# A hybrid decoder layer: the first weight group in a written order, and the stick-breaking heads' last 16 keys in one step

## The chip, the cores and the metric

The kernel runs on one core of a Trainium2 chip. The metric is the device time of one execution, in microseconds (us). Five engines run side by side: TensorE (PE), VectorE (DVE), ScalarE (ACT), GpSimd (POOL) and SyncE (SP, which here only issues DMAs).

## What is computed

One layer over 256 tokens with 16 learned meta tokens in front (T = 272 columns), model width 2048, all in float32:

```
xn = rmsnorm(h) * g_pre;  u = xn @ w_in                  # 5132 columns
mLSTM heads (6), stick-breaking heads (6), pooling (4)   # mixers, from parts of u
h += rmsnorm(concat(mixers) @ w_out);  h += rmsnorm(SwiGLU FFN(h))

stick-breaking, per head:  z = q.k / sqrt(128), keys s < t
A[t,s] = sigmoid(z_ts) * prod_{s<j<t} (1 - sigmoid(z_tj));  out_t = sum_s A[t,s] v_s
```

The keys of a head are the 272 positions, in tiles of 128, 128 and 16. Only the last 16 queries see the last 16 keys.

## The kernel before, in words

**Precision.** Each float32 weight tile is loaded raw and split into a rounded part `hi` (ACT, line 95) and a rest `lo` (DVE, line 96); a product is x_hi·w_hi + x_lo·w_hi + x_hi·w_lo. `mm3` (lines 100 to 102) issues three matmuls into the same columns; `mm2` (lines 545 and 549) takes x_hi and x_lo side by side as one 512-column matmul with `hi`, and one 256-column matmul with `lo`.

**The order of work.** `w_in` is worked through in 11 groups of three or four 128-column blocks (the table `plan`); within a group the 16 k-tiles of 128 rows come in chunks, each loaded by SP into one of three `raw` buffers, split, and multiplied into PSUM banks `acc0` to `acc3`. A block is evacuated when its 16 k-tiles are done. The recording layer schedules PE, ACT and DVE from the program's order. Between the matmuls of the groups `tick()` hands out one step of the heads' own work at a time, with waiting times counted in ticks (`LAG`, `VLAG`); that work uses four other PSUM banks, `mx()`.

**Group 0** (queries of stick-breaking heads 0 to 2, and the 12 gate columns) also makes the transposed x. `x_trans(k)` (lines 222 to 227) transposes one k-tile of the meta tokens `mt` and of both halves of `xin` into a bank; ACT and DVE turn it into `xhi` and `xlo`, scaled by the gain column `gmc`. Eight matmuls on `ones` and the transpose that makes `gmc` (lines 198 and 199) stand ahead of that. The gates use `mm3` with 38 columns of weights `gw` and 272 moving columns, once per k-tile. `x_squares` and `x_norm` make the rms factor `rb`, needed only for evacuation.

**The stick-breaking heads** run in three steps, `LAG` ticks apart: scores (lines 326 to 328, one matmul per key tile, 256, 144 and 16 columns), running sums through the triangle `tri` and `ones_r` (lines 357 to 359, for each of two parts), and weighted values (lines 332 to 334). `vals` (lines 318 to 320) transposes the values, one transpose per key tile. The mLSTM heads use the same `scores`, `weighted` and `vals`.

After `w_in` come the output projection, the FFN's gate and up products, and its down product, with the same splits; they take the time from about 300 us on.

## Time and profile before

| | |
|---|---|
| median of 3 runs | 1117.08 us (1117.01 to 1117.27) |
| profiled execution, its own time | 1117.11 us |
| its span | 1115.4 us |
| PE busy | 1103.0 us |
| DVE busy | 706.8 us |
| ACT busy | 509.6 us |

The span runs from the first to the last instruction; the execution's own time has 1.7 us around it. A line of the timeline gives an instruction's start and its duration. Matmuls overlap in the array, so what one costs PE in a stream is the distance from its start to the next one's, not its duration. The granted clock is given as a share of 2.4 GHz: 1.00 or 0.50 (1.2 GHz).

### The profile page before, as it was taken

How to read it: one execution, taken by the hardware profiler on the slowest of the kernel's cores; microseconds unless marked ns; L12 is line 12 of the kernel's file. 1: busy time of each engine (PE TensorE's matmuls, PEld its weight loads, DVE VectorE, ACT ScalarE, POOL GpSimd, SP SyncE). 2: the span in 40 equal slices, each digit the busy share in tenths (PEclk: the TensorE clock that was granted, in tenths of full speed). 3: DMA queues.
4: the chain of work that ended last, by engine and by line, in shares of the span. 5: the costliest groups of instructions: out<-in, count | busy, mean ns of one | idle time of the engine just before them, and what ended most of it. 6: DMA issues, size and time to landing. Idle time of an engine off the chain costs nothing.

```text
span 1115.4 us, 14181 instructions
## 1 busy us (share of the span) xinstructions
PE 1103.0 (99%) x5671; PEld 943.9 (85%) x5671; DVE 706.8 (63%) x942; ACT 509.6 (46%) x684; POOL 20.5 (2%) x47
## 2 busy tenths in 40 slices
PE   8999999999999999999999999999999999999997
PEld 6899999999988888888888888888888888888885
DVE  4777755868945767576575675774765844454444
ACT  6544455635434654444444444444344543343332
POOL 3000000000000000000000000000000000000000
PEclk8999999999999999999999999999999999999999
DMA  7554644544495555555655555656655565555552
GB/s 245 181 170 151 206 146 130 179 144 128 152 344 194 203 189 189 189 197 182 216 197 189 189 189 190 197 180 208 206 178 199 179 202 190 199 191 198 198 191 75
DMA packets 100545, 208.54 MB, mean 187 GB/s; under 512 B 3962, under 2 KB 31402, under 8 KB 99952
## 3 DMA queue, kind: packets, MB, share of 16 engines
q1 hardware_dynamic: 99168, 201.58, 55.0%
q0 software_dynamic: 896, 2.92, 0.9%
q10 hardware_dynamic: 416, 3.15, 0.7%
q8 instruction: 44, 0.72, 0.3%
q14 instruction: 21, 0.17, 0.0%
HBM read 205.52 MB, written 2.11 MB: 186 GB/s over the span
## 4 chain that ended last, share of the span: by engine, by line
PE 96%; DVE 2%; ACT 1%; DMA 0%; issue 0%; SPq 0%; DVEq 0%; POOLq 0%; ACTq 0%
PE mx L771 8%; PE mx L773 8%; PE mx L772 8%; PE acc L773 7%; PE acc L772 7%; PE acc L771 6%; PE acc L102 5%; PE acc L100 5%; PE acc L101 5%; PE mx L662 5%; PE mx L661 5%; PE mx L663 5%; PE acc L662 5%; PE acc L663 5%; PE acc L661 5%; PE acc L545 4%
## 5 line engine op out<-in xcount | busy, mean ns | idle before, releaser
L96 DVE TENSOR_TENSOR lo<-raw,hi 128x1024 fp32r<-128x1024 f32 (+1 forms) x384 | 458.6, 1200 | 347.4 <-ACT hi L95 345.7
L95 ACT CAST hi<-raw 128x1024 fp32r<-128x1024 f32 (+1 forms) x384 | 394.2, 1030 | 478.9 <-PE mx L773 124.6
L771 PE MATMUL mx<-hi,x 128*128 128x512 f32 x384 | 149.6, 390 | 0.0
L773 PE MATMUL mx<-hi,x 128*128 128x512 f32 x384 | 149.6, 390 | 0.0
L772 PE MATMUL mx<-lo,x 128*128 128x512 f32 x384 | 149.4, 389 | 0.0
L102 PE MATMUL acc<-x,lo 128*128 128x272 f32 (+3 forms) x448 | 132.7, 297 | 0.0
L100 PE MATMUL acc<-x,hi 128*128 128x272 f32 (+3 forms) x448 | 130.5, 292 | 0.1
L101 PE MATMUL acc<-x,hi 128*128 128x272 f32 (+3 forms) x448 | 130.6, 292 | 0.0
L771 PE MATMUL acc<-hi,x 128*128 128x512 f32 x320 | 124.5, 389 | 0.0
L772 PE MATMUL acc<-lo,x 128*128 128x512 f32 x320 | 124.5, 389 | 0.0
L773 PE MATMUL acc<-hi,x 128*128 128x512 f32 x320 | 124.5, 389 | 0.0
L101 PEld LDWEIGHTS acc<-x,hi 128*128 128x128 f32 x448 | 84.4, 188 | 0.7
L100 PEld LDWEIGHTS acc<-x,hi 128*128 128x128 f32 x448 | 84.3, 188 | 0.8 <-DVE sbq L507 0.3
L771 PEld LDWEIGHTS mx<-hi,x 128*128 128x128 f32 x384 | 72.1, 188 | 15.1 <-ACT x L864 0.3
L773 PEld LDWEIGHTS mx<-hi,x 128*128 128x128 f32 x384 | 72.1, 188 | 15.0
L102 PEld LDWEIGHTS acc<-x,lo 128*128 128x128 f32 x448 | 84.4, 189 | 0.4
L772 PEld LDWEIGHTS mx<-lo,x 128*128 128x128 f32 x384 | 72.1, 188 | 14.8
L802 DVE STREAM_TRANSPOSE turn<-hg 32x256 f32<-32x256 f32 x176 | 76.7, 436 | 2.8
L545 PE MATMUL acc<-x,hi 128*128 128x512 f32 x192 | 73.1, 415 | 0.7 <-DVE x L227 0.3
L772 PEld LDWEIGHTS acc<-lo,x 128*128 128x128 f32 x320 | 60.1, 188 | 12.5
L771 PEld LDWEIGHTS acc<-hi,x 128*128 128x128 f32 x320 | 60.1, 188 | 12.5
L773 PEld LDWEIGHTS acc<-hi,x 128*128 128x128 f32 x320 | 60.1, 188 | 12.4
(253 smaller groups left out, 1468.4 us busy)
## 6 DMA issues: line engine op xcount, KB each, us to landing
raw<-in_w_gate_up_dram SPq DMA_DIRECT2D x88, 1024.0 KB, 5.0
raw<-in_w_down_dram SPq DMA_DIRECT2D x44, 1024.0 KB, 5.3
raw<-in_w_in_dram SPq DMA_DIRECT2D x36, 512.0 KB, 4.8
raw<-in_w_out_dram SPq DMA_DIRECT2D x16, 1024.0 KB, 6.0
raw<-in_w_in_dram SPq DMA_DIRECT2D x12, 1024.0 KB, 5.2
raw<-in_w_in_dram SPq DMA_DIRECT2D x8, 768.0 KB, 4.5
raw<-in_w_in_dram SPq DMA_DIRECT2D x3, 792.0 KB, 7.6
h<-in_x_dram ACTq DMA_DIRECT2D x1, 2048.0 KB, 13.2
```

The source lines that it names most:

```text
L95: act.copy(out=h, in_=r)
L96: vec.tensor_tensor(out=l, in0=r, in1=h.bitcast(F32), op=ALU.subtract)
L100: pe.matmul(o, lhsT=wh, rhs=xh, start=start, stop=False, **kw)
L101: pe.matmul(o, lhsT=wh, rhs=xl, start=False, stop=False, **kw)
L102: pe.matmul(o, lhsT=wl, rhs=xh, start=False, stop=stop, **kw)
L545: pe.matmul(o, lhsT=wh, rhs=xx[:, :, k, NMETA:], start=k == 0, stop=k == KT - 1, skip_group_check=True)
L661: pe.matmul(o, lhsT=lh, rhs=h[:, 0, js], start=k == 0, stop=False)
L662: pe.matmul(o, lhsT=lh, rhs=l[:, 0, js], start=False, stop=False)
L663: pe.matmul(o, lhsT=ll, rhs=h[:, 0, js], start=False, stop=k == nk - 1)
L771: pe.matmul(o, lhsT=x2hi[:, k, ts], rhs=h[:, kk, :], start=k == 0, stop=False)
L772: pe.matmul(o, lhsT=x2hi[:, k, ts], rhs=l[:, kk, :], start=False, stop=False)
L773: pe.matmul(o, lhsT=x2lo[:, k, ts], rhs=h[:, kk, :], start=False, stop=k == KT - 1)
```

## The change

**Group 0** is written out by hand (`first_group`), and PE, ACT and DVE keep that order. Its loads have buffers of their own: the three `raw` buffers hold two pairs of k-tiles each, and two of the heads' slots hold the last two pairs. SP issues x and weights in turn, the meta tokens after the sixth; the gain row moves to ACT's queue and `pool_w` behind group 0. The meta tokens are loaded as 128 rows (8 k-tiles by 16 tokens) and transposed twice in all instead of once per k-tile. The gate weights `hi` and `lo` lie side by side, so the gates take two matmuls per k-tile instead of three; ACT and DVE add the parts later. Group 0 is evacuated in the middle of group 1 (`late`), and group 1, now of three blocks, accumulates in three of the four `mx` banks. `mm2` takes `hi` first except in the last k-tile.

**The last 16 keys** of the six stick-breaking heads are gathered by POOL into `q3`, `k3` and `vt3` (96 columns, 16 per head). `last_keys` does their scores and running sums in one step under a block mask, `last_values` one transpose, `last_sums` one product that is added to the heads' last 16 queries. The heads themselves drop their third key tile and subtract the totals `tot3` with one small DVE operation.

```diff
-    chunks = {}
-
-    def load0(a, b):
-        chunks[a] = load(win_view(a, b - a, OG, 396), b - a, 396)
-
-    sp.dma_start(out=row0, in_=g_mix_pre.rearrange("o (a b) -> (o a) b", b=P))
-    load_x(0, 2)
-    sp.dma_start(out=mt, in_=meta)
-    load0(0, 2)
-    load_x(2, 4)
-    load0(2, 4)
-    load_x(4, 8)
-    load0(4, 8)
-    load_x(8, 12)
-    load_x(12, 16)
...
+    raw0 = {}
+    for c in range(3):
+        raw = rawp.tile([P, 2 * MB], F32, tag="raw", name=nm("raw"), bufs=RAWB)
+        for h in range(2):
+            raw0[4 * c + 2 * h] = raw[:, h * 792 : (h + 1) * 792]
+    for h in range(2):
+        raw0[12 + 2 * h] = slots0[1 + h][:, :792]
+    raw0 = {k: r.rearrange("p (k c) -> p k c", c=396) for k, r in raw0.items()}
+
+    def load0(k):
+        sp.dma_start(out=raw0[k], in_=win_view(k, 2, OG, 396))
+
+    act.dma_start(out=row0, in_=g_mix_pre.rearrange("o (a b) -> (o a) b", b=P))
+    for a, b in ((0, 2), (2, 4), (4, 8), (8, 12), (12, 16)):
+        load_x(a, b)
+        for k in range(a, b, 2):
+            load0(k)
+        if b == 8:
+            for h in range(2):
+                sp.dma_start(out=mt8[:, h, :],
+                             in_=meta[:, h * 1024 : (h + 1) * 1024].rearrange("t (k c) -> k t c", c=P))
...
-    pool.dma_start(out=pw, in_=pool_w[0].rearrange("g c d -> c g d"))
...
+    gw = big.tile([P, KT, P], F32R, tag="mixlo", name="gw")
+    pool.memset(gw.bitcast(F32), 0.0)
...
-    pc = mx()
-    for _ in range(8):
-
-        pe.matmul(pc[:, :P], lhsT=ones, rhs=ones, start=True, stop=True)
-    pe.transpose(pc[:, :16], row0, ident[:16, :16])
-    vec.tensor_copy(out=gmc, in_=pc[:, :16])
...
+    def gain_column():
+        pc = mx()
+        warm(pc, 5)
+        pe.transpose(pc[:, :16], row0, ident[:16, :16])
+        vec.tensor_copy(out=gmc, in_=pc[:, :16])
+        warm(pc, 6)
...
-        pe.transpose(pt[:, 0:NMETA], mt[:, ks], ident[:NMETA, :NMETA])
-        pe.transpose(pt[:, NMETA : NMETA + P], xin[:, 0, ks], ident)
-        pe.transpose(pt[:, NMETA + P : T], xin[:, 1, ks], ident)
+        pe.transpose(pt[:, 0:P], xin[:, 0, ks], ident)
+        pe.transpose(pt[:, P : 2 * P], xin[:, 1, ks], ident)
...
-        act.activation(xhi[:, k, :], pt[:, :T], AF.Identity, scale=g)
-        vec.scalar_tensor_tensor(out=xlo[:, k, :], in0=pt[:, :T], scalar=g, in1=xhi[:, k, :].bitcast(F32),
+        act.activation(xhi[:, k, NMETA:], pt[:, :NT], AF.Identity, scale=g)
+        vec.scalar_tensor_tensor(out=xlo[:, k, NMETA:], in0=pt[:, :NT], scalar=g, in1=xhi[:, k, NMETA:].bitcast(F32),
                                  op0=ALU.mult, op1=ALU.subtract)
...
+    def meta_trans():
+        pt = mx()
+        act.activation(jk[:, : 2 * P], mt8.rearrange("p h c -> p (h c)"), AF.Square, accum_out=ssx[:, 2, 0:1])
+        for h in range(2):
+            pe.transpose(pt[:, h * P : (h + 1) * P], mt8[:, h, :], ident)
+        mg = itile(NT).rearrange("p (k t) -> p k t", t=NMETA)
+        vec.tensor_tensor(out=mg, in0=pt[:, : 2 * P].rearrange("p (k t) -> p k t", t=NMETA),
+                          in1=gmc.unsqueeze(2).broadcast_to([P, KT, NMETA]), op=ALU.mult)
+        act.copy(out=xhi[:, :, 0:NMETA], in_=mg)
+        vec.tensor_tensor(out=xlo[:, :, 0:NMETA], in0=mg, in1=xhi[:, :, 0:NMETA].bitcast(F32), op=ALU.subtract)
...
+    def meta_sums():
+        pt = mx()
+        pe.matmul(pt[:NMETA, 0:2], lhsT=sel, rhs=ssx[:, 2, :], start=True, stop=True)
...
+        act.copy(out=e[F], in_=pg[96:102, :T])
+        act.copy(out=ig[:NH], in_=pg[64:70, :T])
...
-        pe.transpose(pv[:, 2 * P : 3 * P], vt[:, K2:T], ident)
-        act.copy(out=dst, in_=pv[:, 0 : 3 * P].rearrange("p (a b) -> p a b", b=P))
...
+        n = dst.shape[1]
+        if n == 3:
+            pe.transpose(pv[:, 2 * P : 3 * P], vt[:, K2:T], ident)
+        act.copy(out=dst, in_=pv[:, 0 : n * P].rearrange("p (a b) -> p a b", b=P))
...
+
+    def scores(k, q, three=True):
         pz = mx()
...
+    have = {"qk": 0, "v": 0, "tot": False, "heads": 0}
+
+    def last_keys():
+        zm, s = zm3[:L16], part3[:L16]
+        pz = mx()
+        pe.matmul(pz[:L16, :L16], lhsT=k3, rhs=q3, start=True, stop=True)
+        vec.tensor_tensor(out=zm, in0=pz[:L16, :L16], in1=sbm3, op=ALU.add)
+        softplus(s, zm)
+        act.copy(out=s3[0], in_=s)
+        vec.tensor_tensor(out=s3[1], in0=s, in1=s3[0].bitcast(F32), op=ALU.subtract)
+        yield
+        pr = mx()
+        for j in range(2):
+            pe.matmul(pr[:, L16 : 2 * L16], lhsT=ones_r[:L16], rhs=s3[j], start=j == 0, stop=False, skip_group_check=True)
+        for j in range(2):
+            pe.matmul(pr[:L16, :L16], lhsT=tri3, rhs=s3[j], start=False, stop=j == 1, skip_group_check=True)
+        vec.tensor_tensor(out=zm, in0=zm, in1=pr[:L16, :L16], op=ALU.subtract)
+        vec.tensor_copy(out=tot3, in_=pr[:, L16 : 2 * L16])
+        act.activation(zm, zm, AF.Exp)
+        have["tot"] = True
+
+    def last_values():
+        pv = mx()
+        pe.transpose(pv[:L16, :P], vt3, ident)
+        vec.tensor_copy(out=v3, in_=pv[:L16, :P])
+        yield
+
+    def last_sums():
+        mhi, mlo_ = mix_tiles()
+        po = mx()
+        pe.matmul(po[:, :L16], lhsT=v3, rhs=zm3[:L16], start=True, stop=True)
+        vec.tensor_tensor(out=part3, in0=po[:, :L16], in1=part3, op=ALU.add)
+        hi, lo = (m[:, NH : 2 * NH, 240:256] for m in (mhi, mlo_))
+        p3 = part3.rearrange("p (h t) -> p h t", t=16)
+        act.copy(out=hi, in_=p3)
+        vec.tensor_tensor(out=lo, in0=p3, in1=hi.bitcast(F32), op=ALU.subtract)
+        ready.update(range(NH, 2 * NH))
+        yield
+
...
-            pe.matmul(pr[:, 0:416], lhsT=tri, rhs=q, start=j == 0, stop=False, skip_group_check=True)
-            pe.matmul(pr[:, 112:256], lhsT=ones_r, rhs=q[:, 256:400], start=False, stop=False, skip_group_check=True)
-            pe.matmul(pr[:, 112:400].rearrange("p (a b) -> p a b", b=144)[:, :, 128:144], lhsT=ones_r,
-                      rhs=q[:, 400:416].unsqueeze(1).broadcast_to([P, 2, 16]), start=False, stop=j == 1,
-                      skip_group_check=True)
-        vec.tensor_tensor(out=zm, in0=zm, in1=pr[:, :416], op=ALU.subtract)
+            pe.matmul(pr[:, 0:400], lhsT=tri, rhs=q, start=j == 0, stop=False, skip_group_check=True)
+            pe.matmul(pr[:, 112:256], lhsT=ones_r, rhs=q[:, 256:400], start=False, stop=j == 1, skip_group_check=True)
+        vec.tensor_tensor(out=zm, in0=zm, in1=pr[:, :400], op=ALU.subtract)
+        z3 = zm[:, 112:400].rearrange("p (a b) -> p a b", b=144)[:, :, 128:144]
+        vec.tensor_tensor(out=z3, in0=z3, in1=tot3[:, h * 16 : h * 16 + 16].unsqueeze(1).broadcast_to([P, 2, 16]),
+                          op=ALU.subtract)
         act.activation(zm, zm, AF.Exp)
         yield
         po = mx()
         v = sbv[h]
-        weighted(po[:, :NT], lambda j: v[:, j, :], zm)
-        act.copy(out=mhi[:, NH + h, :], in_=po[:, :NT])
-        vec.tensor_tensor(out=mlo_[:, NH + h, :], in0=po[:, :NT], in1=mhi[:, NH + h, :].bitcast(F32), op=ALU.subtract)
-        ready.add(NH + h)
+        weighted(po[:, :NT], lambda j: v[:, j, :], zm, three=False)
+
+        act.copy(out=mhi[:, NH + h, :240], in_=po[:, :240])
+        vec.tensor_tensor(out=mlo_[:, NH + h, :240], in0=po[:, :240], in1=mhi[:, NH + h, :240].bitcast(F32), op=ALU.subtract)
+        vec.tensor_copy(out=part3[:, h * 16 : h * 16 + 16], in_=po[:, 240:256])
+        have["heads"] += 1
+        if have["heads"] == NH:
+            quick.append([clock[0] + 4, last_sums(), None])
...
+    def count_qk():
+        have["qk"] += 1
+        if have["qk"] == 2 * NH:
+            quick.append([clock[0] + LAG, last_keys(), None])
...
+                pool.tensor_copy(out=vt3[:, i * 16 : i * 16 + 16], in_=vt[:, NT:T])
+                have["v"] += 1
+                if have["v"] == NH:
+                    quick.append([clock[0] + VLAG, last_values(), None])
...
-        if k == 0:
+        if k < KT - 1:
             high()
...
-        if k:
+        if k == KT - 1:
             high()
...
-        "q0 q1 sbq3 sbq4",
-        "q2 k0 sbq5 sbk0",
-        "k1 k2 sbk1 sbk2",
-        "sbk3 sbk4 sbk5",
+        "q0 q1 sbq3",
+        "q2 k0 sbq4 sbq5",
+        "k1 k2 sbk0 sbk1",
+        "sbk2 sbk3 sbk4 sbk5",
...
+    def first_group(blocks):
+
+        accs, pg = [acc(b) for b in range(3)], acc(3)
+        subs = {}
+
+        def prepare(k):
+            x_trans(k)
+            x_trans(k + 1)
+            subs[k] = split(raw0[k][:, :, 12:], 2, 384)
...
+        def pair(k0):
+
+            h, l = subs[k0]
+            for low in range(2):
+                for b in range(3):
+                    bs = slice(b * P, (b + 1) * P)
+                    for kk in range(2):
+                        k = k0 + kk
+                        if low:
+                            pe.matmul(accs[b][:, :NT], lhsT=l[:, kk, bs], rhs=xhi[:, k, NMETA:], start=False,
+                                      stop=False, skip_group_check=True)
+                        else:
+                            pe.matmul(accs[b], lhsT=h[:, kk, bs], rhs=xx[:, :, k, NMETA:], start=k == 0, stop=False,
+                                      skip_group_check=True)
+            for b in range(3):
+                tick()
+
+        def gate_pair(k0):
+            for k in (k0, k0 + 1):
+                pe.matmul(pg[:102, :T], lhsT=gw[:, k, 0:102], rhs=xhi[:, k, :], start=k == 0, stop=False)
+                pe.matmul(pg[:102, :T], lhsT=gw[:, k, 0:102], rhs=xlo[:, k, :], start=False, stop=k == KT - 1)
+
+        with tc.manual_schedule(engines={mybir.EngineType.PE, mybir.EngineType.Activation, mybir.EngineType.DVE}):
+            gain_column()
+            prepare(0)
+            prepare(2)
+            pair(0)
+            prepare(4)
+            w_gates((0, 2))
+            pair(2)
+            prepare(6)
+            x_squares(0, 0)
+            pair(4)
+            prepare(8)
+            other_cols()
+            meta_trans()
+            w_gates((4, 6))
+            pair(6)
+            prepare(10)
+            x_squares(0, 1)
+            w_gates((8,))
+            pair(8)
+            prepare(12)
+            for k in (0, 2, 4):
+                gate_pair(k)
+            x_squares(1, 0)
+            w_gates((10,))
+            pair(10)
+            prepare(14)
+            x_squares(1, 1)
+            meta_sums()
+            spread = x_norm()
+            w_gates((12, 14))
+            for k in (6, 8, 10):
+                gate_pair(k)
+            pair(12)
+            for b in range(3):
+                products(accs, blocks, b, [(14, subs[14])])
+            spread()
+            gate_pair(12)
+            gate_pair(14)
+        for b in range(3):
+            late.append(lambda b=b: evac(*blocks[b], accs[b]))
+        late.append(lambda: quick.append([0, gates(pg), None]))
+
+    first_group(groups[0])
+    pool.dma_start(out=pw, in_=pool_w[0].rearrange("g c d -> c g d"))
...
+
+        accs = [mx() if gi == 1 else acc(b) for b in range(nb)]
...
+            if ka == 4:
+                while late:
+                    late.pop(0)()
```

The start of TensorE's work in group 0, before: the last x tile that is prepared ahead, and the first weight pair (`hi`, `lo` with `acc` banks).

```order
L222 MATMUL mx_233<-ident,mt 128x16
L223 MATMUL mx_233<-ident,xin 128x128
L224 MATMUL mx_233<-ident,xin 128x128
L545 MATMUL acc_211<-x,hi_243 128x512
L549 MATMUL acc_211<-x,lo_244 128x256 x2
L545 MATMUL acc_211<-x,hi_243 128x512
L545 MATMUL acc_212<-x,hi_243 128x512
L549 MATMUL acc_212<-x,lo_244 128x256 x2
L545 MATMUL acc_212<-x,hi_243 128x512
```

And now:

```order
L255 MATMUL mx_266<-ident,xin 128x128
L256 MATMUL mx_266<-ident,xin 128x128
L763 MATMUL acc_227<-x,hi_257 128x512 x2
L763 MATMUL acc_228<-x,hi_257 128x512 x2
L763 MATMUL acc_229<-x,hi_257 128x512 x2
L760 MATMUL acc_227<-x,lo_258 128x256 x2
L760 MATMUL acc_228<-x,lo_258 128x256 x2
L760 MATMUL acc_229<-x,lo_258 128x256 x2
```

The meta transpose (L222) is gone from each k-tile, and a pair's six `hi` matmuls stand ahead of its `lo` matmuls.

SyncE's queue at the start of the program, before (`row` is the gain, `mt` the meta tokens, `xin` x, `raw` weights):

```order
L147 DMA row_94<-in_g_mix_pre_dram 16x128
L140 DMA xin<-in_x_dram 128x2x256
L149 DMA mt<-in_meta_tokens_dram 16x2048
L87 DMA raw_102<-in_w_in_dram 128x2x396
L140 DMA xin<-in_x_dram 128x2x256
L87 DMA raw_105<-in_w_in_dram 128x2x396
L140 DMA xin<-in_x_dram 128x2x512
L87 DMA raw_108<-in_w_in_dram 128x4x396
L140 DMA xin<-in_x_dram 128x2x512 x2
L87 DMA raw_442<-in_w_in_dram 128x4x396
L87 DMA raw_496<-in_w_in_dram 128x4x396
```

And now (`slot_92` is where the meta tokens go):

```order
L140 DMA xin<-in_x_dram 128x2x256
L153 DMA raw_98<-in_w_in_dram 128x2x396
L140 DMA xin<-in_x_dram 128x2x256
L153 DMA raw_98<-in_w_in_dram 128x2x396
L140 DMA xin<-in_x_dram 128x2x512
L153 DMA raw_99<-in_w_in_dram 128x2x396 x2
L162 DMA slot_92<-in_meta_tokens_dram 128x1x128 x2
L140 DMA xin<-in_x_dram 128x2x512
L153 DMA raw_100<-in_w_in_dram 128x2x396 x2
L140 DMA xin<-in_x_dram 128x2x512
L153 DMA slot_93<-in_w_in_dram 128x2x396
```

Weights follow x directly and the meta tokens come eighth; the gain row is not here any more.

TensorE in the first head's running sums, before (`sh` and `sl` are the two parts, `trio` holds `tri` and `ones_r`):

```order
L357 MATMUL mx_1891<-sh_1773,trio 128x416
L545 MATMUL acc_1849<-x,hi_1853 128x512
L100 MATMUL acc_1846<-x,hi_1857 128x272
L358 MATMUL mx_1891<-sh_1773,trio 128x144
L101 MATMUL acc_1846<-x,hi_1857 128x272
L359 MATMUL mx_1891<-sh_1773,trio 128x2x16
L102 MATMUL acc_1846<-x,lo_1858 128x272
L357 MATMUL mx_1891<-sl_1774,trio 128x416
L100 MATMUL acc_1846<-x,hi_1857 128x272
L358 MATMUL mx_1891<-sl_1774,trio 128x144
L101 MATMUL acc_1846<-x,hi_1857 128x272
L359 MATMUL mx_1891<-sl_1774,trio 128x2x16
```

And now:

```order
L465 MATMUL mx_1894<-sh_1778,trio 128x400
L674 MATMUL acc_1854<-x,lo_1859 128x256
L100 MATMUL acc_1851<-x,hi_1862 128x272
L466 MATMUL mx_1894<-sh_1778,trio 128x144
L101 MATMUL acc_1851<-x,hi_1862 128x272
L465 MATMUL mx_1894<-sl_1779,trio 128x400
L102 MATMUL acc_1851<-x,lo_1863 128x272
L466 MATMUL mx_1894<-sl_1779,trio 128x144
L100 MATMUL acc_1851<-x,hi_1862 128x272
L101 MATMUL acc_1851<-x,hi_1862 128x272
L379 MATMUL mx_1908<-ident,vt_1848 128x128
L102 MATMUL acc_1851<-x,lo_1863 128x272
```

Two of six matmuls (L359) are gone. In their place the six heads share four matmuls, earlier in the program (`s_200` and `s_201` are the two parts for 96 keys):

```order
L428 MATMUL mx_1670<-s_200,trio 128x96
L102 MATMUL acc_1544<-x,lo_1619 128x272
L428 MATMUL mx_1670<-s_201,trio 128x96
L430 MATMUL mx_1670<-s_200,tri_154 96x96
L430 MATMUL mx_1670<-s_201,tri_154 96x96
```

They stand in the stream of group 5.

## Rows read from the trace of the kernel before

**Rows 1.** The page: span, and busy share of each engine.

```profile
span 1115.4 us, 14181 instructions
...
PE 1103.0 (99%) x5671; PEld 943.9 (85%) x5671; DVE 706.8 (63%) x942; ACT 509.6 (46%) x684; POOL 20.5 (2%) x47
```

**Rows 2.** Waits of PE over the span: total us, times, longest.

```profile
PE mx L222 <- DMA mt<-in_meta_tokens_dram: 1.5, 1, 1.5
...
PE mx L223 <- DMA xin<-in_x_dram: 0.7, 1, 0.7
...
PE acc L545 <- DVE im L299: 0.3, 1, 0.3
```

**Rows 3.** Stretches: us, busy by engine, granted clock, DMA share, GB/s.

```profile
7.25:7.50 0.25, 0.25 (x2) 0.13 (x1) 0.00 (x0) 0.00 (x0) 0.25 (x2) 0.86 1.01 360
...
10.00:14.00 4.00, 3.96 (x12) 3.22 (x12) 2.17 (x4) 3.37 (x9) 1.98 (x9) 0.50 1.04 368
...
14.25:42.40 28.15, 28.15 (x176) 22.75 (x177) 19.38 (x48) 21.77 (x57) 0.89 (x1) 1.00 0.67 217
```

**Rows 4.** Timeline of PE in group 0: start, duration, line, shapes, idle before.

```profile
1.13 3.41 PE L198 MATMUL mx<-ones 128*128 128x128 f32 x16 [1.13 <-DVE ssx L210]
...
6.22 0.23 PE L222 MATMUL mx<-ident,mt 16*128 16x16 f32 x1 [1.52 <-DMA mt<-in_meta_tokens_dram]
...
10.04 0.80 PE L545 MATMUL acc<-x,hi 128*128 128x512 f32 x1 [0.34 <-DVE x L227]
...
14.36 0.33 PE L223 MATMUL mx<-ident,xin 128*128 128x128 f32 x1
14.52 0.27 PE L224 MATMUL mx<-ident,xin 128*128 128x128 f32 x1
14.73 0.23 PE L222 MATMUL mx<-ident,mt 16*128 16x16 f32 x1
...
16.35 0.39 PE L545 MATMUL acc<-x,hi 128*128 128x512 f32 x1
...
16.70 0.39 PE L545 MATMUL acc<-x,hi 128*128 128x512 f32 x1
...
37.14 0.93 PE L242 MATMUL mx<-im,ones 128*128 128x128 f32 x6
...
42.25 0.29 PE L102 MATMUL acc<-x,gw 128*38 128x272 f32 x1
42.38 0.28 PE L100 MATMUL acc<-x,hi 128*128 128x260 f32 x1
```

**Rows 5.** All five loads of x: us from issue to landing.

```profile
DMA to landing us min/median/max: 3.9/7.8/10.3
```

**Rows 6.** SyncE timeline, the first load of x and of weights: issue time, duration.

```profile
1.26 0.40 SPq L140 DMA_DIRECT2D xin<-in_x_dram  x1
...
2.21 0.42 SPq L87 DMA_DIRECT2D raw<-in_w_in_dram  x1
```

**Rows 7.** Timeline of ACT: first cast of a weight tile, first four-tile evacuation.

```profile
7.62 0.83 ACT L95 CAST hi<-raw 128x768 fp32r<-128x768 f32 x1 [5.53 <-DMA raw<-in_w_in_dram]
...
14.83 2.09 ACT L226 ACTIVATE x<-mx,gmc 128x272 fp32r<-128x272 f32 x4 [1.40 <-PE mx L224]
```

**Rows 8.** Timeline of PE in the stick-breaking stage, columns as in rows 4.

```profile
154.01 0.29 PE L328 MATMUL mx<-sbq,sbk 128*128 128x16 f32 x2
...
154.35 0.29 PE L102 MATMUL acc<-x,lo 128*128 128x272 f32 x1
...
158.38 0.27 PE L320 MATMUL mx<-ident,vt 128*128 128x128 f32 x1
...
158.62 0.29 PE L102 MATMUL acc<-x,lo 128*128 128x272 f32 x1
...
164.13 0.18 PE L359 MATMUL mx<-sh,trio 128*128 128x32 f32 x1
...
164.36 0.35 PE L357 MATMUL mx<-sl,trio 128*128 128x416 f32 x1
```

More of the change, by code (lines that the diff above doesn't have):

```diff
@@ L110, in tile_hybrid_layer @@
     vec.memset(neghalf, -0.5)
-    act.preload_act_table_set("natural_log_exp_and_others")
     def inv_rms(dst, ss, n):
@@ L199, in tile_hybrid_layer, with warm @@
-    pe.transpose(pc[:, :16], row0, ident[:16, :16])
-    vec.tensor_copy(out=gmc, in_=pc[:, :16])
+    def warm(pc, n):
+        for _ in range(n):
+            pe.matmul(pc[:, P : 2 * P], lhsT=ones, rhs=ones, start=True, stop=True)
+    def gain_column():
[4 more added lines that the diff above has]
+        warm(pc, 6)
     C_GF, C_PS, C_CW = 0, 16, 20
@@ L246, in tile_hybrid_layer, with spread @@
+        def spread():
+            pr = mx()
+            for (j, n, d), a in zip(dg, (NMETA, NMETA + P, 0)):
+                pe.matmul(pr[:, a : a + n], lhsT=ones[:n, :], rhs=d[:n, :n], start=True, stop=True)
+            vec.tensor_copy(out=rb, in_=pr[:, :T])
+        return spread
     sbq = [mp.tile([P, NT], F32, name=f"sbq{h}") for h in range(NH)]
     sbk = [mp.tile([P, T], F32, name=f"sbk{h}") for h in range(NH)]
-    sbv = [mp.tile([P, 3, P], F32, name=f"sbv{h}") for h in range(NH)]
+    sbv = [mp.tile([P, 2, P], F32, name=f"sbv{h}") for h in range(NH)]
@@ L249, in tile_hybrid_layer @@
+    q3, k3, vt3, zm3, tot3, part3 = (mp.tile([P, L16], F32, name=n) for n in ("q3", "k3", "vt3", "zm3", "tot3", "part3"))
+    s3 = [mp.tile([P, L16], F32R, name=f"s3{j}")[:L16] for j in range(2)]
+    v3 = mp.tile([P, P], F32, name="v3")[:L16]
     mlq = [mp.tile([P, NT], F32, name=f"mlq{h}") for h in range(NH)]
@@ L341, in two_parts, with softplus @@
         return h, l
-    def stick(h, w):
-        mhi, mlo_ = mix_tiles()
-        pz = scores(sbk[h], sbq[h])
-        zm, s = w[:, 0:416], w[:, 416:832]
-        vec.tensor_tensor(out=zm, in0=pz[:, :416], in1=sbm, op=ALU.add)
+    def softplus(s, zm):
         act.activation(s, zm, AF.Abs)
@@ new lines, in products @@
+    def products(accs, blocks, b, subs):
+        kind, i = blocks[b]
+        ts = slice(first(kind, i), T)
+        bs = slice(b * P, (b + 1) * P)
+        for k0, (h, l) in subs:
+            for kk in range(2):
+                k = k0 + kk
+                if ts.start == NMETA:
+                    mm2(accs[b], h[:, kk, bs], l[:, kk, bs], k)
+                else:
+                    mm3(accs[b][:, : T - ts.start], h[:, kk, bs], l[:, kk, bs], xhi[:, k, ts], xlo[:, k, ts],
+                        k == 0, k == KT - 1)
+            tick()
```

176 lines of the change are left out of this document (84 added, 92 removed).

## The prediction

> **What bounds the kernel now.** I read the page first: PE is busy 1103.0 of 1115.4 us, DVE and ACT far less [rows 1]. So only what PE no longer does, no longer waits for, or does at a higher clock can shorten the time; work taken from ACT, DVE or POOL counts only where PE waits for it. The list of PE's waits comes second: all that it names at the start sum to some 3 us, and behind them stands one wait of 0.3 us for the gates' evacuation, where group 1 wants a bank that group 0 still holds [rows 2]. From the first weights on, then, PE is a queue without gaps, and the price of an instruction is the distance between starts.
>
> Third, the stretches [rows 3]: the granted clock falls to 0.50 at about 7.4 us and comes back at 14.25; before the fall PE had stood idle for 1.5 us and then waited again for x [rows 2, 4]. From 14.25 to the end of group 0 PE is busy for 28.15 of 28.15 us at the full clock. Fourth, the timeline of PE in group 0: first product at 10.04, first product of group 1 at 42.38 [rows 4]. Group 0 is where the change can take most, as the end of group 0 moves everything behind it.
>
> **Group 0, worked out anew.** I do not subtract from the old 42.38 but add up the new stream, since the start, the order and the clock all change.
>
> Work of PE at the full clock, from the first product on:
> - Products: a `hi` and a `lo` matmul together take 0.35 (16.35 to 16.70) [rows 4]; 16 k-tiles by 3 blocks, 48 x 0.345 = 16.6 us. The new order inside a pair changes no count.
> - Transposes: the change drops the meta transpose of each k-tile. Two transposes of x cost 2 x 0.16 = 0.33 (14.36 to 14.52 [rows 4]; with the step back to the next one 0.37). Four k-tiles are prepared ahead, 12 remain: 4.0 us.
> - Gates: two instead of three matmuls per k-tile, 32 x 0.125 = 4.0 us (42.25 to 42.38 is one [rows 4]); the third one's 16 x 0.125 = 2.0 us is gone. 102 instead of 38 weight columns move no more columns.
> - The rest: two meta transposes 0.37, the column tile and the sum for the meta rows 0.2 each, the spreading of the norm 0.93 [rows 4]: 1.7 us.
>
> Together 26.3 us. Start: the quickest load of x takes 3.9 us [rows 5], which must be the first, so it landed at 1.26 + 3.9 = 5.2 [rows 6]; it is now first in SP's queue, so some 4.8. The first weights, issued at 2.21, were cast from 7.62, when their load released ACT [rows 6, 7]. They are now issued some 0.9 us sooner with one load of 0.13 MB fewer before them: between 6.3 and 7.2. The second x, 0.26 MB later at 368 GB/s [rows 3], lands between 7.0 and 7.9; its four transposes take 0.66. The first pair starts between 7.4 and 8.5, I take 7.8, and at the full clock group 0 would end at 34.1.
>
> The clock: the 11 `ones` matmuls now span the gap better (8 took 3.41 us [rows 4]), but PE still waits for both x loads, about as long as before, so I let the clock fall again at 7.4. Behind 7.8, however, PE works without the gaps that it had up to 10.04. The low stretch was 6.85 us long; its bounds are zero and the same end as before, 14.25, and I take half: it ends at about 11 and costs (11 - 7.8) / 2 = 1.6 us (bounds 0 and 3.2). So group 1 starts at 35.7 instead of 42.4: **6.7 us** (bounds 4.5 and 9).
>
> What covers this: per pair PE needs 2.7 us (2.07 of products, 0.66 of transposes). ACT needs two evacuations at 0.52 and one cast at 0.83 [rows 7], 1.9 us, in four of eight pairs also a square of 1024 columns (768 of the cast take 0.83, so some 1.1); over eight pairs 20 against 26. DVE was busy 19.4 of 28.15 us in the same work [rows 3] and gets a little less. The transposes stand one pair ahead of their products, so ACT's 1.9 has 2.7 to fit in. Data: 5.5 MB at 368 GB/s are 15 us, the last weights land at about 20, and are wanted after 29. If that cover goes, the price is in the second rival.
>
> **Moves with one answer.** SP's queue loses the gain row (now on ACT's queue, where only the table load stands behind it) and takes the meta tokens eighth; all of group 0's loads have buffers, so none waits for a split. `pool_w` goes behind group 0 on POOL's queue and is wanted at the end of `w_in`. The memset of `gw` moves ahead of the masks on POOL, 10 us before its first reader. The copies into `q3`, `k3`, `vt3` are 18 small POOL operations beside a PE that has no use for them until eight ticks later. Zero each. Group 1 in the `mx` banks no longer waits for group 0's banks: **0.3 us** [rows 2]. The regrouping of `plan` keeps every block.
>
> **The last 16 keys.** The price of a small instruction is the distance from its start to that of the instruction after the next, less the 0.125 of the group's matmul in between [rows 8]:
> - scores, two passes of 16 columns (L328): 154.35 - 154.01 - 0.125 = 0.215; the weighted values (L334) have the same form: 12 x 0.215 = 2.6 us for six heads;
> - running sums (L359): 164.36 - 164.13 - 0.125 = 0.105, twice per head: 1.3 us;
> - third value transpose (L320): 158.62 - 158.38 - 0.125 = 0.115, six times: 0.7 us.
>
> That is 4.6 us removed. Added: two float32 products of 96 columns at some 0.23, four matmuls of 96 columns at 0.11 and one transpose at 0.115 (the same rows; they are a little wider than the small ones), 1.0 us. The net is **3.6 us** (bounds 2.8 and 4.2). The steps of `last_keys` lie eight ticks apart, some 6 us of PE's own work, for seven operations on 96 columns; the heads need their result only a group later. The extra DVE operations per head (a 32-column subtraction, a 16-column copy) have DVE's idle third to lie in [rows 1].
>
> **Sum.** 6.7 + 0.3 + 3.6 = 10.6 us. The profiled execution took 1117.11 us, 1.7 of it around the span, and equals the median of the runs (1117.08). 1117.1 - 10.6 = **1106.5 us**.
>
> **Rivals.**
> 1. *The clock*, both ways. If PE's transposes and `ones` matmuls keep it up, the 1.6 us fall away: 1104.9. If it comes back at 14.25 as before, another 1.6 us are lost: 1108.1. For the one speaks that PE's idle time before 7.4 is a little shorter, for the other that rows 3 show no earlier return. Chance 0.13 each.
> 2. *Slower: the written order makes a chain of what overlapped.* PE, ACT and DVE now keep a fixed order in group 0; if PE finds each pair's tiles unready, it waits for transposes, two evacuations (1.04), a cast (0.83) and the `lo` split (taken at the cast's 0.83) one after the other, 2.7 us in each of the seven pairs behind the first: 19 us. The time would be 1106.5 + 19 = 1125.5. It makes the kernel slower once a pair waits over 1.5 us (10.6 / 7). Against it: the order puts each tile's preparation a pair ahead, and neither engine is full. 0.02; as much for waits that just eat the gain, 1117.
> 3. *Small matmuls were nearly free.* If a small matmul cost only its columns, at 0.125 per 272 [rows 8], the six heads would give 0.7 us and take 0.4: the last keys would bring 0.3 instead of 3.6, and the time would be 1109.8. Rows 8 speak against it: the group's own matmul is held up each time. 0.08.
>
> The Trainium skill has a rule on the side of the third rival, in "TensorE: Matmul & The Clock Gate", section "Back-to-back issue gap": up to 64 columns a matmul takes a floor of about 25 ns between starts. By that, 36 small matmuls were worth 0.9 us, and the sum would be near 1109. The trace differs: 0.105 us and more for each matmul with its own weights.
>
> **How the numbers follow.** The forecast has 0.62, the clock 0.26, cheap small matmuls 0.08, the two cases of waits 0.04. The range takes in the clock both ways, with the bounds of start and small matmuls beside it, and most of the third rival: 1103.8 to 1109.4. A measurement of this kernel can tell about 0.2%, 2.2 us, from no change. All cases but the two of waits are faster by more than that: 0.96 faster, 0.02 the same, 0.02 slower.
>
> **What would show it.** In the timeline of PE the first product stands near 7.8 and group 1's first near 35.7 (over 38: a wait or the clock; the stretches and the waits tell which). The granted clock is low from about 7.4 to 11. No line of gates has 38 columns, and between 140 and 215 us PE stays full. Behind group 0 every stage is earlier by the same amount, and by 3.6 us more once the heads are through. I am wrong if PE's waits in group 0 exceed 3 us, if DVE or ACT is what PE waits for there, or if the stage of the heads shows new waits for `tot3` or `part3`.

## The result, and the profile after

The changed kernel takes 1107.61 us in the median (1106.81 to 1108.28); the kernel before took 1117.17 in the same runs. The ratio is 0.9913 [0.9901, 0.9925]: faster by 9.6 us, against 10.6 forecast. The profiled execution after took 1108.28 us, 8.8 less than the one of before.

The page after has PE as full as before [rows 1], in less time:

```profile
span 1106.6 us, 14131 instructions
...
PE 1094.2 (99%) x5616; PEld 939.0 (85%) x5616; DVE 709.0 (64%) x961; ACT 505.5 (46%) x671; POOL 28.7 (3%) x70
```

PE's waits, as in [rows 2]. The waits for the meta tokens, for x and for the gates' evacuation are gone; the longest line is new:

```profile
PE acc L100 <- DVE sig L655: 1.3, 2, 0.9
...
PE acc L763 <- ACT hi L95: 0.4, 1, 0.4
```

PE's timeline in group 0, which answers to [rows 4]:

```profile
4.11 0.26 PE L228 MATMUL mx<-ident,slot 16*128 16x16 f32 x1 [0.47 <-DMA slot<-in_g_mix_pre_dram]
4.63 2.93 PE L223 MATMUL mx<-ones 128*128 128x128 f32 x12 [0.27 <-DVE gmc L229]
7.35 0.42 PE L255 MATMUL mx<-ident,xin 128*128 128x128 f32 x1
7.57 0.42 PE L256 MATMUL mx<-ident,xin 128*128 128x128 f32 x1
...
9.70 2.12 PE L763 MATMUL acc<-x,hi 128*128 128x512 f32 x6 [0.43 <-ACT hi L95]
11.66 0.86 PE L760 MATMUL acc<-x,lo 128*128 128x256 f32 x6
12.36 0.27 PE L255 MATMUL mx<-ident,xin 128*128 128x128 f32 x1
12.47 0.27 PE L256 MATMUL mx<-ident,xin 128*128 128x128 f32 x1
...
35.45 0.28 PE L100 MATMUL mx<-x,hi 128*128 128x260 f32 x1
```

ACT's timeline ahead of the first product:

```profile
8.02 0.90 ACT L258 ACTIVATE x<-mx,gmc 128x256 fp32r<-128x256 f32 x2 [5.45 <-PE mx L256]
8.82 0.82 ACT L95 CAST hi<-raw 128x768 fp32r<-128x768 f32 x1
```

Two things are to be read here. Group 1 starts at 35.45, close to the forecast (35.7), but the first product stands at 9.70 instead of 7.8: six `ones` matmuls fill 4.63 to 7.35 ahead of the x transposes, and behind the first two transposes ACT evacuates two k-tiles and casts the first weights, one after the other, until 9.64. And the x transposes are 0.21 apart at 7.35, 0.11 apart from 12.36 on; before they cost 0.16 each, with a small meta transpose between them.

Landmarks of PE's timelines, in us from the start of each span, show where the 8.8 us come from and where some of it goes. The last two columns are experiments 1 and 8 below.

| first instruction of | before | after | earlier by | group 0 alone (1) | loads later (8) |
|---|---|---|---|---|---|
| group 1 | 42.38 | 35.45 | 6.9 | 35.26 | 35.13 |
| the last stick-breaking head's weighted values, second tile | 206.69 | 196.19 | 10.5 | 199.04 | 195.86 |
| a product of `w_in` just ahead of the new wait (L102) | 221.62 | 210.42 | 11.2 | 213.96 | 210.09 |
| the sixth such product behind it | 224.01 | 214.65 | 9.4 | 216.35 | 212.48 |
| the mLSTM heads' scores | 248.79 | 239.44 | 9.4 | 241.15 | 237.27 |
| gate and up products | 386.10 | 377.02 | 9.1 | 378.50 | 374.62 |
| down product | 866.95 | 857.87 | 9.1 | 859.33 | 855.46 |
| (span) | 1115.4 | 1106.6 | 8.8 | 1108.7 | 1104.1 |

The two rows with products compare the same ones, counted back from the end of `w_in` (the 109th and the 103rd L102 of 272 columns). Ahead of the new wait PE is 11.2 us ahead, 4.2 us of its time later only 9.4: the wait costs 1.8 us. PE's timeline before:

```profile
221.62 0.29 PE L102 MATMUL acc<-x,lo 128*128 128x272 f32 x1
...
224.01 0.29 PE L102 MATMUL acc<-x,lo 128*128 128x272 f32 x1
```

Timeline of DVE there, after:

```profile
201.72 0.91 DVE L519 SCALAR_TENSOR_TENSOR slot<-slot,ucol,mlm 128x256 f32<-128x256 f32 x3 [3.66 <-DMA slot<-M_d]
...
207.76 0.42 DVE L655 TENSOR_TENSOR sig<-acc,sig 128x256 f32<-128x256 f32 x1
...
209.57 1.75 DVE L548 RECIPROCAL sig<-sig 128x256 f32<-128x256 f32 x1
211.24 0.36 DVE L655 TENSOR_TENSOR sig<-acc,sig 128x256 f32<-128x256 f32 x1
...
213.45 0.41 DVE L655 TENSOR_TENSOR sig<-acc,sig 128x256 f32<-128x256 f32 x1
```

PE's timeline at the same place, after:

```profile
210.42 0.29 PE L102 MATMUL acc<-x,lo 128*128 128x272 f32 x1
211.65 0.39 PE L100 MATMUL acc<-x,hi 128*128 128x272 f32 x1 [0.94 <-DVE sig L655]
...
213.92 0.40 PE L100 MATMUL acc<-x,hi 128*128 128x272 f32 x1 [0.36 <-DVE sig L655]
...
214.65 0.29 PE L102 MATMUL acc<-x,lo 128*128 128x272 f32 x1
```

The idle times sum to 1.3 us only, since idle time counts from the end of the matmul before, and in a stream the next one would have started earlier than that (0.125 us behind the start of the last).

The additions of line 655 empty the banks of the output-gate blocks o2 to o5, which group 8 needs. On DVE they stand behind the first decay matrices of the mLSTM heads (line 519), and those wait 3.66 us for the load of `M_d` into a slot which a stick-breaking head has just left.

### The profile page after: what moved, and what is told of

It reads as the page before. It is cut to its first block, busy times and chain, and to the rows that moved or that the text cites. A ratio compares the mean times of both kernels' runs of the same rounds, so it can differ in the third digit from the quotient of the medians.

```text
span 1106.6 us, 14131 instructions
## 1 busy us (share of the span) xinstructions
PE 1094.2 (99%) x5616; PEld 939.0 (85%) x5616; DVE 709.0 (64%) x961; ACT 505.5 (46%) x671; POOL 28.7 (3%) x70
## 4 chain that ended last, share of the span: by engine, by line
PE 95%; DVE 3%; DMA 1%; ACT 1%; issue 0%; DVEq 0%; POOLq 0%; ACTq 0%
PE mx L953 8%; PE mx L955 8%; PE mx L954 8%; PE acc L955 7%; PE acc L954 7%; PE acc L953 7%; PE mx L844 5%; PE mx L845 5%; PE mx L843 5%; PE acc L844 5%; PE acc L845 5%; PE acc L102 4%; PE acc L100 4%; PE acc L843 4%; PE acc L101 4%; PE acc L670 2%
## 5 line engine op out<-in xcount | busy, mean ns | idle before, releaser
L102 PE MATMUL acc<-x,lo 128*128 128x272 f32 (+3 forms) x416 | 123.4, 297 | 0.0
L100 PE MATMUL acc<-x,hi 128*128 128x272 f32 (+3 forms) x416 | 121.9, 293 | 1.3 <-DVE sig L655 1.3
L101 PE MATMUL acc<-x,hi 128*128 128x272 f32 (+3 forms) x416 | 121.1, 291 | 0.0
L100 PEld LDWEIGHTS acc<-x,hi 128*128 128x128 f32 x416 | 78.3, 188 | 2.6 <-DVE sig L655 1.7
L102 PEld LDWEIGHTS acc<-x,lo 128*128 128x128 f32 x416 | 78.4, 189 | 0.3
L101 PEld LDWEIGHTS acc<-x,hi 128*128 128x128 f32 x416 | 78.4, 189 | 0.1
L670 PE MATMUL acc<-x,hi 128*128 128x512 f32 x134 | 48.4, 395 | 0.0
```

Source lines behind the costliest of these rows:

```text
L100: pe.matmul(o, lhsT=wh, rhs=xh, start=start, stop=False, **kw)
L101: pe.matmul(o, lhsT=wh, rhs=xl, start=False, stop=False, **kw)
L102: pe.matmul(o, lhsT=wl, rhs=xh, start=False, stop=stop, **kw)
```

## The experiments

Four questions: what each part brings alone, whether the new wait is what the heads' part gave back, what the small transposes and the written order are worth, and why the first product is late. The kernel before was timed again beside each set of runs (medians 1116.83 to 1117.15). The numbers are those of the runs; there is no 5.

**1 and 2. Each part alone.** Experiment 1 is the changed kernel with the heads as before; experiment 2 is the kernel before with the heads' part.

Of experiment 1, against the changed kernel:

```diff
-    sbv = [mp.tile([P, 2, P], F32, name=f"sbv{h}") for h in range(NH)]
+    sbv = [mp.tile([P, 3, P], F32, name=f"sbv{h}") for h in range(NH)]
...
-            count_qk()
...
```

Of experiment 2, against the kernel before:

```diff
-        vec.tensor_tensor(out=zm, in0=zm, in1=pr[:, :416], op=ALU.subtract)
+        vec.tensor_tensor(out=zm, in0=zm, in1=pr[:, :400], op=ALU.subtract)
+        z3 = zm[:, 112:400].rearrange("p (a b) -> p a b", b=144)[:, :, 128:144]
...
```

> The group 0 part of the change with the heads' third key tile left as before. If the two parts add up, group 1 starts at 35.4 us as in the changed kernel, PE has no wait for the o blocks' evacuation (DVE and PE stand to each other as before), and the time is 1117.2 - 7.2 = 1110.0 us. Rival: the wait of 1.3 us comes from group 0 being earlier, not from the shorter heads: then it is here too and the time is near 1111.

> The heads' last 16 keys in one step, group 0 and the table of groups as before. If small matmuls cost what the timeline of before says, PE loses 3.6 us of work, and if the new wait belongs to this part, 1.3 us of it come back as a wait of TensorE for the evacuation of the o blocks: 1114.8 us. Rival (small matmuls nearly free): 1116.5. Rival (wait belongs to group 0): no such wait, 1113.6.

Group 0 alone: 1109.36 us, ratio 0.9932 [0.9918, 0.9945], a gain of 7.5. The heads alone: 1115.52 (11 runs, 1115.04 to 1117.97), ratio 0.9992 [0.9983, 1.0001], at most a small gain. That time lies between the 1114.8 expected and the 1116.5 of nearly free matmuls, so the timeline has to decide. In experiment 1 PE has no wait for `sig`, although the same chain stands on DVE (the first decay matrix waits 3.05 us for `M_d`); in experiment 2 PE has one of 1.0 us, in the list of its waits:

```profile
PE acc L100 <- DVE sig L614: 1.0, 2, 0.6
```

So the wait comes with the heads' part, whatever group 0 does. In experiment 2 the product just ahead of the wait is 3.65 us earlier than before (217.97 against 221.62), close to the 3.6 forecast; the one behind it is 2.15 earlier, and 1.4 are left at the gate and up products (384.68 against 386.10). The median of the spans is 1.7 us shorter than before (1113.4 against 1115.1), that of the times only 1.3: its executions take 2.1 us around the span, against 1.7 before; why is not shown.

Against experiment 1, PE in the changed kernel comes to this place 3.5 us sooner (210.42 against 213.96), but the first of the four additions only 1.5 (207.76 against 209.27).

**3. The decay matrices eight ticks later.**

```diff
         pool.dma_start(out=pb, in_=M_d[h : h + 1].broadcast_to([P, 2, NT]))
         yield
+        yield
```

> The changed kernel with the mLSTM heads' first computing step eight ticks later, so that DVE no longer stands 3.7 us in front of the load of a slot from M_d ahead of its splits. If that standing is what makes the evacuation of the o blocks late, TensorE's wait of 1.3 us for it goes and the time is about 1106.3. Rival: the two reciprocals of 1.75 us ahead of those additions alone set it; then the wait stays and so does 1107.6.

1108.7 us, ratio 0.9928 [0.9916, 0.9941]: a miss. The recording layer's scheduler put line 519's operations (520 there) where they had been (201.50); only the later steps moved. The wait for `sig` stayed (1.4 us), and the output projection now waits 1.0 us for the pooling's operand. It tells nothing about the theory.

**4. Without the second run of `ones` matmuls.**

```diff
         vec.tensor_copy(out=gmc, in_=pc[:, :16])
-        warm(pc, 6)
```

> The changed kernel without the second run of six ones matmuls, which ended at 7.35 us when x had been in for some 1.5 us. The first x transposes can start near 6 us, the first product near 8.4 instead of 9.7. If the clock comes up at the same time as before (10.7 us), group 1 starts 0.7 us sooner: 1106.9. Rival: the six matmuls are what brings the clock up at 10.7; without them it comes later, up to 14 us, and group 1 starts up to 1 us later: 1108.6.

1107.44 us, ratio 0.9912 [0.9899, 0.9926], no different from the change, but the timeline of PE is:

```profile
4.47 0.47 PE L254 MATMUL mx<-ident,xin 128*128 128x128 f32 x1
...
6.58 0.47 PE L254 MATMUL mx<-ident,xin 128*128 128x128 f32 x1 [0.98 <-DMA xin<-in_x_dram]
...
7.34 2.91 PE L762 MATMUL acc<-x,hi 128*128 128x512 f32 x6
```

The first x was there at 4.5 and the first product starts at 7.34 (8.4 expected): in the change the six `ones` held it back. Six products take 2.91 us here and 1.66 in experiment 12, at the full pace, so much of that start is spent at half of it. Group 1 starts at 34.50, 0.95 sooner; at the gate and up products 0.4 of it are left, and the wait for `sig` is 1.8 instead of 1.3 us. That this place eats what PE gains ahead of it is not shown by that: in experiments 6 and 7, where group 1 starts 4.9 and 4.7 us later than in the change, the wait is 1.4 and 1.6 us.

**6 and 7. The small transposes, and the written order.** Experiment 6 puts a 16-row transpose ahead of each two x transposes (its result is not used). Experiment 7 leaves group 0's order to the scheduler.

```diff
         ks = slice(k * P, (k + 1) * P)
+        pe.transpose(pt[:, 2 * P : 2 * P + 16], row0, ident[:16, :16])
         pe.transpose(pt[:, 0:P], xin[:, 0, ks], ident)
```

```diff
-        with tc.manual_schedule(engines={mybir.EngineType.PE, mybir.EngineType.Activation, mybir.EngineType.DVE}):
+        if True:
```

> The changed kernel with one 16-row, 16-column transpose per k-tile put back ahead of the two x transposes (its result is not used): the price of the meta transposes that the change dropped. If a small transpose costs its own start only (0.11 to 0.13 us): 12 of them at the full clock, 1.5 us, and four at the low clock, 0.8, hidden or not: time 1109 to 1110. If it also makes the two x transposes dearer, as the distances of before (0.54 for the three, against 0.22 for the two now) suggest: 12 x 0.32 = 3.8 us and more at the start: 1111.5 or above. If PE has slack there after all: 1107.6.

> The changed kernel with the order of group 0 left to the scheduler: the same instructions, loads and buffers, but no order by hand for PE, ACT and DVE. If the gain of group 0 is in the work removed, the earlier loads and their own buffers, group 1 starts within 1 us of 35.45 and the time is 1107 to 1109. If the written order is what keeps PE full (each pair's preparation ahead of its products), PE waits in group 0 for evacuations or splits, 2 us or more in sum, and the time is 1110 or above.

Experiment 6: 1113.12 us, ratio 0.9956 [0.9942, 0.9969]; three of its five runs take 1113.1 to 1113.6, two 1110.7, and the profiled one is of the three. Group 1 starts at 40.37. Its timeline of PE shows one k-tile in 0.54 (13.58 to 14.12), where the change takes 0.22:

```profile
13.58 0.23 PE L255 MATMUL mx<-ident,slot 16*128 16x16 f32 x1
13.75 0.33 PE L256 MATMUL mx<-ident,xin 128*128 128x128 f32 x1
13.91 0.27 PE L257 MATMUL mx<-ident,xin 128*128 128x128 f32 x1
14.12 0.23 PE L255 MATMUL mx<-ident,slot 16*128 16x16 f32 x1
```

The timeline of PE's weight loads, same kernel:

```profile
13.80 0.14 PEld L257 LDWEIGHTS mx<-ident,xin 128*128 128x128 f32 x1
14.12 0.13 PEld L255 LDWEIGHTS mx<-ident,slot 16*128 16x128 f32 x1 [0.17 <-issue]
14.28 0.14 PEld L256 LDWEIGHTS mx<-ident,xin 128*128 128x128 f32 x1
```

The 16-row load takes no longer than a full one (0.13), but begins only at 14.12, 0.32 behind the load before it, with the loader idle for 0.17; in the change the loads of full transposes follow each other every 0.11. What holds the small load back is not shown. The Trainium skill ("TensorE: Matmul & The Clock Gate", section "LDWEIGHTS (loading the stationary operand)") says that a load's time goes by its columns and not by its rows; the durations agree, the distances are what that rule leaves out. By the distances, and by the median, the second case of the expectation holds: in the profiled execution sixteen such transposes go with a start of group 1 that is 4.9 us later (40.37 against 35.45). Of these, 12 x 0.32 = 3.8 us are their price at the full clock; 0.5 is the clock, which came up later (six products take 2.66 us at the start instead of 2.12), and 0.6 the later first product (10.30). What made two runs 2.4 us shorter is open, as neither was profiled.

Experiment 7: 1113.29 us, ratio 0.9966 [0.9952, 0.9979], group 1 at 40.12. Its timeline of PE, then of DVE:

```profile
3.81 0.48 PE L255 MATMUL mx<-ident,xin 128*128 128x128 f32 x1
10.29 2.93 PE L223 MATMUL mx<-ones 128*128 128x128 f32 x12 [6.01 <-DVE gmc L229]
```

```profile
6.51 0.96 DVE L96 TENSOR_TENSOR lo<-raw,hi 128x768 fp32r<-128x768 f32 x1 [5.40 <-ACT hi L95]
8.80 1.07 DVE L96 TENSOR_TENSOR lo<-raw,hi 128x768 fp32r<-128x768 f32 x1 [1.33 <-ACT hi L95]
...
10.08 0.16 DVE L229 COPY gmc<-mx 128x16 f32<-128x16 f32 x1
```

The scheduler put two weight splits, which wait for ACT's casts of weights still to land, ahead of a copy that was ready at 4; PE waits 6.0 us for it. That one place is what the written order saves. The time is that of the second case of the expectation, but its reason, waits for evacuations or splits, is not: from the first product to group 1 both streams take the same (25.6 and 25.75 us), so the order of the pairs themselves shows no gain.

**8, 9 and 11. The wait for `sig` taken away.** A copied column makes the first three `M_d` loads wait until o5 is evacuated, so that the scheduler places line 519 behind the four additions. Experiment 8 is the change with that; experiment 9 also lacks the six `ones`, as in 4; experiment 11 is experiment 1 with it.

```diff
         pb = w[:, 416:928].rearrange("p (a t) -> p a t", t=NT)
+        if h < 3:
+            pool.tensor_copy(out=pb[:, 0, 0:1], in_=mlo_of(5)[:, 0:1])
```

> The changed kernel, with the M_d loads of the first three mLSTM heads placed behind the evacuation of block o5 (a copy of one column of o5's tile into the load's target), so that the decay matrices that wait 3.7 us for the load on DVE no longer stand ahead of the four additions of the o blocks. Theory (the 1.3 us that PE lost to those additions are what the heads' part gave back): the wait of PE for sig falls from 1.3 us to 0.3 or less, the first mLSTM scores on PE come near 238.1 instead of 239.4, the span near 1105.3, the time near 1106.3. Rival (DVE is simply full there, 3.8 of 4 us in two stretches, so another instruction becomes the late one): the wait stays at 1 us or more, or an equal one appears at the mLSTM scores, and the time stays near 1107.6.

> The last one with the second run of six ones matmuls taken out as well. In the run without those six, group 1 started 0.95 us earlier (34.50), but only 0.4 us of it were left at the first product of w_out, and PE's wait for sig grew from 1.3 to 1.8 us. Theory (that wait is the one place where an earlier PE loses what it gained): both gains add up, first product of w_out near 374.8, span near 1104.4, time near 1105.4. Rival (DVE is the bound between 200 and 215 us): the 0.95 us is lost again, time near 1106.5 or above.

> The group 0 part alone (heads as before) with the first three M_d loads behind the evacuation of o5, as in the run with 1105.79. In the run of the group 0 part alone PE had no wait for sig, so with it the loads' place should bring nothing, and the difference to 1105.79 is what the heads' part is worth when the wait is gone. Theory (the heads' part removes the 3.6 us forecast and its shortfall was that wait): 1109.4, within 0.5 us. Rival (the late load cost PE something there as well, and the heads' part really is worth about 2): 1107.5 to 1108.

Experiment 8: 1105.79 us, ratio 0.9899 [0.9886, 0.9913]. No wait for `sig` is left, and on DVE's timeline the additions begin 2.3 us sooner:

```profile
204.31 1.23 DVE L96 TENSOR_TENSOR lo<-raw,hi 128x1024 fp32r<-128x1024 f32 x1 [1.58 <-ACT hi L95]
205.45 0.42 DVE L657 TENSOR_TENSOR sig<-acc,sig 128x256 f32<-128x256 f32 x1
...
208.96 0.36 DVE L657 TENSOR_TENSOR sig<-acc,sig 128x256 f32<-128x256 f32 x1
```

DVE is still busy for 4.00 of 4 us from 208 to 212 there, so being full was not the cause; what stood first was. DVE still waits for an `M_d` load, 4.28 us until 225.09, with none of the four additions behind it, and PE loses nothing. The intervals of this run and of the change overlap (1.8 us between the medians); what rests on the traces does not depend on them: the products ahead of and behind that place are 11.5 us earlier than before, both. Experiment 11: 1109.6, ratio 0.9935 [0.9923, 0.9948], as experiment 1. With the wait gone, then, the heads' part brings 1109.6 - 1105.8 = 3.8 us (by the ratios 4.0): the 3.6 forecast. Products at equal place agree: behind the heads PE is 7.7 us ahead in experiment 1 and 11.5 in experiment 8. Experiment 9: 1105.23, ratio 0.9894 [0.9881, 0.9908], 0.6 below 8, where the intervals overlap. It does not tell whether the 0.95 us of experiment 4 can be kept, as its group 1 starts only 0.29 sooner than that of 8 (34.84 against 35.13): in 8 PE's pace came up earlier. (The "first product of w_out" of its expectation is the first of the gate and up products.)

**10 and 12. The start.** Experiment 10 is 9 with the gain row first in SP's queue; experiment 12 is 8 with PE's two gaps before the x transposes filled.

```diff
-    act.dma_start(out=row0, in_=g_mix_pre.rearrange("o (a b) -> (o a) b", b=P))
+    sp.dma_start(out=row0, in_=g_mix_pre.rearrange("o (a b) -> (o a) b", b=P))
```

```diff
-        pc = mx()
-        warm(pc, 5)
+        pw1, pc = mx(), mx()
+        warm(pw1, 7)
...
-        warm(pc, 6)
+        warm(pw1, 6)
```

> The run with 1105.23 (no second run of ones matmuls, M_d loads behind o5) with the gain row first in SP's queue instead of ACT's. If ACT's queue was what made the row late (it was used 3.3 us after its issue), it is there at about 3.2 and the x transposes of the first load start near 4.4 all the same, as x itself lands then; x and the weights are issued some 0.5 us later, so the second x load, for which PE waited 1.3 us, comes later by as much: first product near 8.0 instead of 7.55, time 1105.2 to 1105.8. Rival: the row ahead of x costs nothing and the first transposes start earlier: 1104.8.

> The run with 1105.79 with PE's two short gaps at the start filled: seven instead of five ones matmuls before the gain row, and the ones matmuls in a bank of their own, so that the six behind don't wait for the copy of the gain column. It asks what PE's work before the first products does to its clock there. If the gaps held the clock down: the spacing of the x transposes is 0.11 from the first one on, the first product near 9.0, group 1 near 34.3, time near 1105. If they did not: x transposes 0.21 apart until 8 us or later as in the two runs so far, group 1 between 34.9 and 35.5, and 1105.8.

Experiment 10: 1105.46 us, ratio 0.9895 [0.9880, 0.9911]; PE has the gain row at 3.56 and waits 1.8 us for x instead of 1.3. Its first product starts at 7.58, as in 9 (7.55), not at the 8.0 expected. The row's queue decides nothing. Experiment 12: 1105.31, ratio 0.9897 [0.9884, 0.9911]. Its timeline of PE:

```profile
1.13 3.36 PE L223 MATMUL mx<-ones 128*128 128x128 f32 x14 [1.13 <-DVE s L243]
4.42 0.28 PE L228 MATMUL mx<-ident,slot 16*128 16x16 f32 x1
4.63 1.86 PE L223 MATMUL mx<-ones 128*128 128x128 f32 x12
6.33 0.27 PE L255 MATMUL mx<-ident,xin 128*128 128x128 f32 x1
6.43 0.27 PE L256 MATMUL mx<-ident,xin 128*128 128x128 f32 x1
...
8.35 1.66 PE L765 MATMUL acc<-x,hi 128*128 128x512 f32 x6 [0.85 <-ACT hi L95]
```

The first case of the expectation holds: with no gap, the second run of `ones` takes 1.86 instead of 2.93 us, the x transposes are 0.11 apart from the first one, and group 1 starts at 33.65, 1.5 sooner than in 8. PE keeps these 1.5 us until the last mLSTM head (278.06 against 279.52) and has 0.6 of them at the gate and up products (374.00 against 374.62). Between the two PE stands idle ahead of the transposes of the normalized h:

```profile
368.74 0.41 PE L1044 MATMUL acc<-ident,h 128*128 128x128 f32 x2 [1.18 <-issue]
```

In experiment 8 the same gap is 0.26 us. These transposes need `h`, which DVE finishes (from 368.16) behind two weight splits and the row sums; the splits follow ACT's casts, and those wait 2.00 us for a load of `w_gate_up`. That the next bound lies there was read, not tried.

## Why the prediction was right, and where not

**What bounds it.** Right: what PE no longer does or waits for came out of the time. The sum was near (10.6 forecast, 9.6 measured), in part by luck: errors within its terms cancel.

**Group 0, 6.7 us: 6.9 measured, by two wrong steps that cancel.** "The first pair starts between 7.4 and 8.5, I take 7.8" was wrong; it was 9.70. The step worked the start out from x and the weights alone and gave the six `ones` matmuls behind the gain row no time; PE takes them in order, at half its later pace, ahead of the x transposes (without them the first product starts at 7.34, experiment 4). It also left out the two evacuations and the cast on ACT between transposes and product: PE waits 0.4 us for that cast. A wait for ACT in group 0 was one of the prediction's own signs of being wrong; it came, small. Against that stood "two transposes of x cost 2 x 0.16": they cost 0.22 together, since 0.16 was the price beside a 16-row transpose (experiment 6). Over 12 k-tiles that is 1.3 us less for PE. The rest is the clock: behind 9.70 the low pace cost only some 0.5 us of the 1.6 reckoned (9.70 to 11.66 against 8.35 to 9.85 in experiment 12), as the pace came up near 10.7, close to the 11 assumed: the six `lo` products from 11.66 take 0.70, as later ones do. But the course that the prediction gave for it, a granted clock that falls at 7.4 and is low until 11, did not occur: it reads 1.00 throughout group 0, and the pace was low from the start. The gates cost 0.125 each, as priced.

**The last 16 keys, net 3.6: right as PE's work, some 1.8 too much as time.** Experiments 8 and 11 give 3.8. What failed is that PE "stays full" between 140 and 215 us. The extra DVE operations do "have DVE's idle third to lie in" (experiment 8 keeps them, and PE waits for none), but that average hid a stretch in which DVE's order matters: with 3.5 us less work PE reached the banks of o2 to o5 before DVE had emptied them. The wait cost PE 1.8 us (1.3 of them shown as idle), and taking it away brought 1.8 in the median.

**Group 1 in other banks.** Right: the wait of 0.3 us is gone. In experiment 1 the lead grows from 7.1 us at group 1 to 7.7 at the table's product; what brings the other 0.3 was not looked into.

**The rivals.** The written order makes no chain beyond that 0.4 us, and removes one at the start (experiment 7, 6.0 us at one place). Small matmuls are not nearly free: the 3.8 us stand by the distances of [rows 8], against the 0.3 of that rival, and against the floor between starts that the Trainium skill gives ("TensorE: Matmul & The Clock Gate", section "Back-to-back issue gap"). The same section says that in a stream of loads and matmuls both set the spacing; the trace agrees with that, as each of these matmuls has weights of its own. The clock: the pace came up at different times, with the same instructions ahead of it; see below.

## What to carry to other kernels

When a stage loses work on the engine that bounds it, look at the in-order engines which empty its buffers: a step that waits for a load, placed ahead of an evacuation, can cost nothing until the bounding engine gets a few us faster. Price an instruction in the company that it will have: two full transposes cost 0.11 each alone and 0.16 beside a 16-row one. And work put in to warm an engine up stands in its queue like any other: here its second run delayed the first product by 2.4 us, and without it the kernel was no slower (experiments 4 and 9).
